# Moving the small tiles of a decoder kernel into an SBUF pool of their own, so that all large tiles start at multiples of 64 bytes

## The chip, the cores and the metric

The kernel runs on one core of one Trainium2 chip. The metric is the device time of one execution in microseconds; three executions of the kernel before gave a median of 2481.26 us (2479.68 to 2482.8).

## The reference

A small decoder: one retention layer and one latent-attention layer, each followed by a squared-ReLU MLP, for 256 tokens of width 2048 in float32. Of its work nearly all is in large matrix products with weights that are read once from HBM:

```python
def retention(h, w_in, w_out, cos, sin):
    ...
    proj = h @ w_in
    q, k, v, gate = jnp.split(proj, [H * dk, 2 * H * dk, 2 * H * dk + H * dv], axis=-1)
    ...
    return (jax.nn.silu(gate) * o) @ w_out
...
def sq_relu_mlp(h, w1, w2):
    return jnp.square(jax.nn.relu(h @ w1)) @ w2
...
    for layer in range(DEPTH):
        if layer < N_A_LAYERS:
            h = rms_norm(x, norm_mix[layer])
            x = x + retention(h, ret_w_in[layer], ret_w_out[layer], ret_cos, ret_sin)
        else:
            j = layer - N_A_LAYERS
            if j == 0:
                k_nope, k_pe, v = mla_shared_kv(rms_norm(x, kv_norm_in), mla_w_kv_down, mla_kv_norm,
                                                mla_w_kv_up, mla_k_nope_norm, mla_k_pe_norm,
                                                mla_cos, mla_sin)
            h = rms_norm(x, norm_mix[layer])
            x = x + mla_attention(h, mla_w_dq[j], mla_q_norm[j], mla_w_uq[j], mla_q_nope_norm[j],
                                  mla_q_pe_norm[j], mla_w_o[j], k_nope, k_pe, v, mla_cos, mla_sin)
        x = x + sq_relu_mlp(rms_norm(x, norm_mlp[layer]), mlp_w1[layer], mlp_w2[layer])
    return x
```

`w_in` is 2048 x 12288, `w_out` 4096 x 2048, each MLP 2048 x 8192 and 8192 x 2048. The rotary tables, the retention's decayed scores and the softmax attention are in the parts left out.

## The kernel before

**Number format.** TensorE multiplies in fp32r. To keep float32 accuracy each operand is split into a high part and the rest (`split`): ScalarE rounds (`CAST` to `wh`), VectorE subtracts (`TENSOR_TENSOR` to `wl`), and a product is three matmuls: high by high, high by low, low by high. Activations are split the same way into tiles called `act` (their names in the profile: a, y, n, hid, ckv, cq, ot, and those with `_more` for sums).

**Stages in order.** Retention: eight heads, each with the projections rq, rk (`gemm_t`) and rg, rv or rp (gate and value), then the output product ro; MLP 0 (u is the product with w1, d the one with w2); the shared keys and values kd, ku; the query products dq, dqp, uq; the attention output wo, wop; MLP 1 (u and d again). Most products are 2x2 block products (`gemm_pair`, `quad`). Some chunks of them use seven products instead of eight, with sums of weights that VectorE makes into buffers `us` (u_u, d_u, rp_u).

**Flow of the weights.** Each chunk of 1 MB goes by a DMA that SyncE issues into one of three `raw` buffers of 8 KB per partition, is split half by half into one of five `wh` and one of five `wl` buffers of 4 KB, and is used from there. `wh` and `wl` are the *moving* operand of the matmul, 512 columns at a time; a 128 x 128 piece of an `act` tile is the *stationary* one, its weights. In `gemm_t` it is the other way round: there `act` moves.

**What sets the order.** All operations are recorded first (`Plan.record`); a list scheduler then puts them in order by cost tables and due times, chooses buffers, and emits them all from one line, L421. So every instruction of the profile carries L421 and is told apart by tile names.

**Where tiles lie.** `nc.tile` makes a tile only when its first instruction is emitted. A tile with a tag gets one of the tag's buffers; each buffer is a slot of the SBUF pool, and slots follow each other in the order of their first use, each rounded up to 32 bytes. In the kernel before, one pool `sb` holds everything: the large tiles, the 36 small buffers of 32 bytes (`small`), and odd ones: `gains` (392 bytes), `pos_i` and `pos_f` (8 bytes), `neg_half` (64 bytes), `gqn` (4 bytes). So the large slots start at multiples of 32 bytes, and some 32-byte slots between them shift what follows.

Of the kernel before, what the change touches and what calls it, by code (L numbers as in the profile page):

```python
# [11 lines left out]
F32 = mybir.dt.float32  # L12
F32R = mybir.dt.float32r
BF16 = mybir.dt.bfloat16
I32 = mybir.dt.int32
# [436 lines left out]
P = 128  # L452
NT = 2
# [17 lines left out]
G_CKV, G_CQ, G_KN, G_QN, G_ALL = 80, 84, 96, 97, 98  # L471
# [6 lines left out]
def _pi_parts():  # L478
    two_pi = 2 * PI
    c1 = round(two_pi * 2**9) / 2**9  # L480
    c2 = round((two_pi - c1) * 2**23) / 2**23
    return c1, c2, two_pi - c1 - c2
# [3 lines left out]
def yoco(ctx: ExitStack, tc: tile.TileContext, a):  # L486
    nc = Plan(tc.nc, tc)
    pool = ctx.enter_context(tc.tile_pool(name="sb", bufs=1))
    psum = ctx.enter_context(tc.tile_pool(name="ps", bufs=1, space=PSUM))

    def f2k(shape, name, dtype=F32):
        return nc.tile(pool, [P, *shape], dtype, name, "f2k", 14)

    def small(w, name):
        return nc.tile(pool, [P, w], F32, name, "small", 36)

    def shaped(t, shape):
        v = t[:, : math.prod(shape)]
# [32 lines left out]
            run_first()  # L531


    gains = nc.tile(pool, [P, G_ALL], F32, "gains")
    cst = nc.tile(pool, [P, C_ALL], F32, "cst")
    pos_i = nc.tile(pool, [P, NT], I32, "pos_i")
    gpe = nc.tile(pool, [P, 2 * ROPE], F32, "gpe")
    nc.scalar.dma_start(gains, a["gains"])
    ident = cst[:, C_ID : C_ID + P]
    mask = cst[:, C_MASK : C_MASK + 3 * P]  # L540
    neg_half = nc.tile(pool, [P, 16], F32, "neg_half")
    nc.gpsimd.memset(neg_half, -0.5)
    warm = small(1, "warm")
    nc.scalar.copy(warm, neg_half[:, 0:1])

# [61 lines left out]
    def rstd(total, n, w, name):  # L607

        m = small(w, f"{name}_m")
        nc.gpsimd.tensor_scalar(m, total, 1.0 / n, EPS, op0=ALU.mult, op1=ALU.add)  # L610
        r = small(w, f"{name}_r")
        nc.gpsimd.tensor_tensor(r, m, neg_half[:, :w], op=ALU.pow)
        return r
# [363 lines left out]


    c1, c2, c3 = _pi_parts()
    pos_f = nc.tile(pool, [P, NT], F32, "pos_f")  # L980

    def sincos(inv, w, name):

# [43 lines left out]
    scale = (NOPE + ROPE) ** -0.5  # L1027
    rope_tab = nc.tile(pool, [P, 2, S], F32, "rope_tab")
    pe_tabs = [[nc.tile(pool, [P, 2, ROPE], F32, f"petab{t}{i}") for i in range(2)] for t in range(NT)]
    gqn = nc.tile(pool, [P, 1], F32, "gqn")  # L1030

    def mla_tables():
        sm = mla_sc[0](no_turn[0])
# [698 lines left out]
```

## Time and profile before

| | |
|---|---|
| Median of three executions | 2481.26 us |
| The profiled execution | 2479.39 us |
| Its span, first to last instruction | 2477.6 us |
| ScalarE busy | 1739.1 us (70%) |
| GpSimd busy | 248.1 us (10%) |
| Granted TensorE clock | 0.999 |
| HBM read, written | 479.14 MB, 39.85 MB |

"Busy" is the time in which an engine runs an instruction. For TensorE the ends of matmuls are modelled and they overlap: the page gives a 512-column matmul some 395 ns, though the next one begins much sooner. The pace of TensorE is therefore read from starts, that is from the count of matmuls in a stretch of time. PE is the matmul itself, PEld the loading of its weights.

### The profile page before, as it was taken

How to read it: one execution, taken by the hardware profiler on the slowest of the kernel's cores; microseconds unless marked ns; L12 is line 12 of the kernel's file. 1: busy time of each engine (PE TensorE's matmuls, PEld its weight loads, DVE VectorE, ACT ScalarE, POOL GpSimd, SP SyncE). 2: the span in 40 equal slices, each digit the busy share in tenths (PEclk: the TensorE clock that was granted, in tenths of full speed). 3: DMA queues.
4: the chain of work that ended last, by engine and by line, in shares of the span. 5: the costliest groups of instructions: out<-in, count | busy, mean ns of one | idle time of the engine just before them, and what ended most of it. 6: DMA issues, size and time to landing. Idle time of an engine off the chain costs nothing.

```text
span 2477.6 us, 31762 instructions
## 1 busy us (share of the span) xinstructions
PE 2465.7 (100%) x11406; PEld 2035.9 (82%) x11406; DVE 2240.7 (90%) x2959; ACT 1739.1 (70%) x2457; POOL 248.1 (10%) x287
## 2 busy tenths in 40 slices
PE   9999999999999999999999999999999999999999
PEld 7888888888888888888888788998888788888887
DVE  6899999888899999999999998777899899999999
ACT  6666666666667858668668777677678677586684
POOL 6510001000000010010110001111000100100100
PEclk9999999999999999999999999999999999999999
DMA  9566679666565697696887555445556976977874
GB/s 336 187 196 214 197 209 243 199 201 217 197 235 196 202 259 229 205 263 201 235 274 207 196 201 186 156 147 178 202 206 200 251 224 209 261 224 213 263 235 156
DMA packets 143742, 533.12 MB, mean 215 GB/s; under 512 B 61152, under 2 KB 62560, under 8 KB 90336
## 3 DMA queue, kind: packets, MB, share of 16 engines
q1 hardware_dynamic: 122192, 484.90, 58.7%
q0 software_dynamic: 21248, 46.15, 9.6%
q8 instruction: 89, 1.46, 0.2%
q14 instruction: 69, 0.57, 0.1%
q10 hardware_dynamic: 144, 0.05, 0.0%
HBM read 479.14 MB, written 39.85 MB: 209 GB/s over the span
## 4 chain that ended last, share of the span: by engine, by line
PE 96%; DVE 2%; DMA 1%; ACT 1%; issue 1%; SPq 0%; DVEq 0%; ACTq 0%
PE d_c L421 20%; PE u_c L421 20%; PE rp_c L421 8%; PE u_p L421 7%; PE ro_c L421 6%; PE d_p L421 6%; PE uq_acc L421 4%; PE rk_acc L421 4%; PE rq_acc L421 4%; PE rp_p L421 3%; PE ku_acc L421 2%; PE wo_acc L421 2%; PE ro_p L421 1%; PE wop_c L421 1%; PE dqp_c L421 1%; PE rg_acc L421 1%
## 5 line engine op out<-in xcount | busy, mean ns | idle before, releaser
L421 PE MATMUL d_c<-d_wh,hid 128*128 128x512 f32 x1412 | 464.4, 396 | 0.0
L421 PE MATMUL u_c<-u_wh,n 128*128 128x512 f32 x1328 | 435.6, 394 | 0.0
L421 PEld LDWEIGHTS d_c<-d_wh,hid 128*128 128x128 f32 x1412 | 265.2, 188 | 62.3 <-ACT d_wh L421 0.2
L421 PEld LDWEIGHTS u_c<-u_wh,n 128*128 128x128 f32 x1328 | 249.3, 188 | 58.2
L421 ACT CAST u_wh<-u_raw 128x1024 fp32r<-128x1024 f32 (+1 forms) x256 | 237.4, 952 | 79.8 <-PE u_c L421 59.6
L421 DVE TENSOR_TENSOR d_wl<-d_raw,d_wh 128x1024 fp32r<-128x1024 f32 (+1 forms) x256 | 281.4, 1110 | 6.2 <-ACT d_wh L421 5.6
L421 DVE TENSOR_TENSOR u_wl<-u_raw,u_wh 128x1024 fp32r<-128x1024 f32 (+1 forms) x256 | 275.3, 1095 | 10.6 <-ACT u_wh L421 9.6
L421 PE MATMUL d_c<-d_wl,hid 128*128 128x512 f32 x706 | 278.7, 395 | 0.0
L421 ACT CAST d_wh<-d_raw 128x1024 fp32r<-128x1024 f32 (+1 forms) x256 | 242.2, 966 | 33.4 <-PE d_c L421 17.4
L421 PE MATMUL u_c<-u_wl,n 128*128 128x512 f32 x664 | 261.7, 394 | 1.0 <-DVE u_wl L421 1.0
L421 ACT CAST d_wh<-d_u 128x1024 fp32r<-128x1024 f32 x106 | 108.5, 1048 | 142.5 <-DVE d_u L421 140.6
L421 ACT CAST u_wh<-u_u 128x1024 fp32r<-128x1024 f32 x120 | 123.7, 1051 | 97.1 <-DVE u_u L421 77.8
L421 PE MATMUL rp_c<-rp_wh,a 128*128 128x512 f32 x560 | 183.0, 393 | 0.0
L421 DVE TENSOR_TENSOR u_wl<-u_u,u_wh 128x1024 fp32r<-128x1024 f32 x120 | 143.9, 1221 | 23.8 <-ACT u_wh L421 23.8
L421 PEld LDWEIGHTS d_c<-d_wl,hid 128*128 128x128 f32 x706 | 132.7, 188 | 31.5 <-DVE d_wl L421 0.7
L421 PEld LDWEIGHTS u_c<-u_wl,n 128*128 128x128 f32 x664 | 124.7, 188 | 30.3 <-DVE u_wl L421 1.5
L421 ACT CAST rp_wh<-rp_raw 128x1024 fp32r<-128x1024 f32 x112 | 103.5, 943 | 62.7 <-PE rp_c L421 36.7
L421 DVE TENSOR_TENSOR d_wl<-d_u,d_wh 128x1024 fp32r<-128x1024 f32 x106 | 126.8, 1221 | 14.3 <-ACT d_wh L421 14.3
L421 DVE TENSOR_TENSOR rp_wl<-rp_raw,rp_wh 128x1024 fp32r<-128x1024 f32 x112 | 119.6, 1094 | 7.4 <-ACT rp_wh L421 7.0
L421 PEld LDWEIGHTS rp_c<-rp_wh,a 128*128 128x128 f32 x560 | 105.1, 188 | 24.8 <-DVE rk_u L421 0.9
L421 PE MATMUL u_p<-u_wh,n_more 128*128 128x512 f32 x360 | 122.6, 395 | 0.0
L421 PE MATMUL ro_c<-ro_wh,y 128*128 128x512 f32 x368 | 120.0, 396 | 0.0
(479 smaller groups left out, 5946.3 us busy)
## 6 DMA issues: line engine op xcount, KB each, us to landing
u_raw<-in_mlp_w SPq DMA_DIRECT2D x128, 1024.0 KB, 6.2
d_raw<-in_mlp_w SPq DMA_DIRECT2D x128, 1024.0 KB, 5.0
rp_raw<-in_ret_w_gv SPq DMA_DIRECT2D x56, 1024.0 KB, 5.1
ro_raw<-in_ret_w_out SPq DMA_DIRECT2D x32, 1024.0 KB, 5.3
uq_raw<-in_mla_w_uq SPq DMA_DIRECT2D x24, 768.0 KB, 4.2
rq_raw<-in_ret_w_qk SPq DMA_DIRECT2D x16, 1024.0 KB, 6.2
rk_raw<-in_ret_w_qk SPq DMA_DIRECT2D x16, 1024.0 KB, 4.9
xh<-d_c POOLq DMA_DIRECT2D x48, 256.0 KB, 6.3
```

The lines of the kernel that those rows point to most:

```text
L421: op.made = fn(*(real(v) for v in op.args), **{k: real(v) for k, v in op.kw.items()})
```

## The change

It makes a second pool `few` for the 36 small buffers and for `pos_i`, `pos_f`, `neg_half` and `gqn`, and makes `gains` 112 columns wide instead of 98 (448 bytes instead of 392), of which the added 14 are not used:

```diff
     pool = ctx.enter_context(tc.tile_pool(name="sb", bufs=1))
+    few = ctx.enter_context(tc.tile_pool(name="few", bufs=1))
...
     def small(w, name):
-        return nc.tile(pool, [P, w], F32, name, "small", 36)
+        return nc.tile(few, [P, w], F32, name, "small", 36)
...
-    gains = nc.tile(pool, [P, G_ALL], F32, "gains")
+    gains = nc.tile(pool, [P, G_ALL + 14], F32, "gains")
     cst = nc.tile(pool, [P, C_ALL], F32, "cst")
-    pos_i = nc.tile(pool, [P, NT], I32, "pos_i")
+    pos_i = nc.tile(few, [P, NT], I32, "pos_i")
...
-    nc.scalar.dma_start(gains, a["gains"])
+    nc.scalar.dma_start(gains[:, :G_ALL], a["gains"])
...
-    neg_half = nc.tile(pool, [P, 16], F32, "neg_half")
+    neg_half = nc.tile(few, [P, 16], F32, "neg_half")
...
-    pos_f = nc.tile(pool, [P, NT], F32, "pos_f")
+    pos_f = nc.tile(few, [P, NT], F32, "pos_f")
...
-    gqn = nc.tile(pool, [P, 1], F32, "gqn")
+    gqn = nc.tile(few, [P, 1], F32, "gqn")
```

The built program has the same instructions in the same order on every engine, with the same waits; the two differ in addresses alone. The byte in its partition at which each large slot starts, in both built programs (in brackets: modulo 256):

| Slots | Before | After |
|---|---|---|
| raw | 20704 (224), 33056 (32), 57632 (32) | 20672, 32960, 57536 (192 each) |
| wh | 43296 (32), 67872 (32), 86848 (64), 99136 (64), 111424 (64) | 43200, 67776, 86720, 99008, 111296 (192 each) |
| wl | 53536 (32), 76064 (32), 90944 (64), 103232 (64), 119616 (64) | 53440, 75968, 90816, 103104, 119488 (192 each) |
| us | 183296 (0), 187392 (0) | 182976, 187072 (192 each) |
| act, 24 slots | 2 at (32), 6 at (64), 6 at (96), 2 at (0), 1 at (128), 7 at (192) | 24 at (192) |
| f2k, 14 slots | 1 at (0), 7 at (32), 6 at (96) | 14 at (192) |

Within a slot a matmul's moving operand starts at a multiple of 2,048 bytes and its stationary one at a multiple of 512.

## The prediction

> **What bounds the kernel now.** I read the page first, then the list of TensorE's waits, then the busy time in stretches of 60 us, and at last short stretches in which every matmul has its operands in known places.
>
> ```profile
> span 2477.6 us, 31762 instructions
> PE 2465.7 (100%) x11406; PEld 2035.9 (82%) x11406; DVE 2240.7 (90%) x2959; ACT 1739.1 (70%) x2457; POOL 248.1 (10%) x287
> PE 96%; DVE 2%; DMA 1%; ACT 1%; issue 1%; SPq 0%; DVEq 0%; ACTq 0%
> ...
> PE idle L421 <- DVE zeros L421: 1.2, 1, 1.2
> PE u_c L421 <- DVE u_wl L421: 1.0, 1, 1.0
> PE rg_acc L421 <- ACT a L421: 0.9, 1, 0.9
> PE d_p L421 <- DVE n L421: 0.7, 1, 0.7
> ```
>
> TensorE is busy for 2465.7 of 2477.6 us and holds 96% of the chain that ended last; its longest wait for anyone is 1.2 us (columns: total us, times, longest). So TensorE's own pace sets the time, and a change counts by what it does to the distance from one matmul to the next. Nearly all of that work is of one form: 9,412 matmuls of 512 columns in fp32r, 8,883 of which have neighbours of the same form (the built program counts them). The other 529 alternate with 256-column ones in the rq and rk projections.
>
> **What the change can touch.** No instruction is added, removed or moved, and no wait changes. Only start addresses do. VectorE and ScalarE show no sign of caring: the raw buffers never begin at a multiple of 64 bytes before the change, the buffers called u always do, and the same operation takes the same time from either.
>
> ```profile
> L421 DVE TENSOR_TENSOR d_wl<-d_raw,d_wh 128x1024 fp32r<-128x1024 f32 x203 | 245.0, 1221 | 6.2 <-ACT d_wh L421 5.6
> L421 DVE TENSOR_TENSOR d_wl<-d_u,d_wh 128x1024 fp32r<-128x1024 f32 x106 | 126.8, 1221 | 14.3 <-ACT d_wh L421 14.3
> L421 ACT CAST d_wh<-d_raw 128x1024 fp32r<-128x1024 f32 x203 | 210.8, 1056 | 32.4 <-PE d_c L421 17.1 <-issue 7.8 <-ACT d_wh L421 3.5
> L421 ACT CAST d_wh<-d_u 128x1024 fp32r<-128x1024 f32 x106 | 108.5, 1048 | 142.5 <-DVE d_u L421 140.6 <-PE d_c L421 0.8
> ```
>
> 1221 against 1221 ns, and 1056 against 1048. For the two elementwise engines I take zero; the bound from these rows is 8 ns on a cast, and ScalarE, 70% busy, would hide that. The 36 small tiles, pos_i, pos_f, gqn and neg_half are read as scalars beside long work; their move I cost at nothing too.
>
> TensorE is another matter. While a matmul streams its moving operand, the weights of the next one are being loaded:
>
> ```profile
> 880.07 0.39 PE L421 MATMUL d_c<-d_wl,hid 128*128 128x512 f32 x1
> 880.07 0.42 PEld L421 LDWEIGHTS d_c<-d_wh,hid 128*128 128x128 f32 x2
> ```
>
> Both begin at 880.07. So I compared, for every matmul, where its moving operand starts with where the *next* one's weights start. Before the change the difference modulo 256 bytes is 0 for 1,707 of the 8,883, 64 for 387, 128 for 1,400, 192 for 1,077, and no multiple of 64 for 4,312. The windows view shows unbroken stretches of one kind (columns: stretch, sum, busy us of PE with its matmul records, clock, DMA share, GB/s; x counts also the records still running at the edges). By the trace's own start times the numbers that begin inside them are, in this order, 29 and 29 (difference 0), 21 (the end of the first of these), 36 and 26 (no multiple of 64), 26 (128), 24 (192) and 24 (64).
>
> ```profile
> 801.21:807.81 6.60, 6.60 (x30) 1.00 0.73 206
> 2428.33:2434.93 6.60, 6.60 (x30) 1.00 0.68 223
> 803.05:807.81 4.76, 4.76 (x22) 1.00 0.85 260
> 251.72:260.12 8.40, 8.40 (x38) 1.00 0.60 157
> 2419.25:2425.31 6.06, 6.06 (x28) 1.00 0.56 181
> 344.23:350.29 6.06, 6.06 (x27) 1.00 0.56 188
> 899.15:904.74 5.59, 5.59 (x26) 1.00 0.89 223
> 2353.71:2359.20 5.49, 5.49 (x25) 1.00 0.90 316
> ```
>
> Divide: 6.60/29 = 227.6 ns where the two starts agree, and 4.76/21 = 226.7 once such a stretch has run for eight matmuls. 8.40/36 = 233.3, 6.06/26 = 233.1, 6.06/26 = 233.1 and 5.59/24 = 232.9 for the other kinds, 5.49/24 = 228.8 for a difference of 64. The granted clock is 1.00 in all of them, so it is no throttle, and the stretches lie in early and late stages alike. All stretches of at least 12 matmuls say the same: 49 with difference 0 lie around 228.1 ns, 231 of the three slow kinds around 233. After the change the built program has difference 0 in all 8,883 places: the pool rounds slots to 32 bytes, every size left in it is a multiple of 64 and the long ones of 512, so everything large starts at 192 modulo 256. That is more than the change's words say.
>
> **The sum.** Slow kinds: 4,312 + 1,400 + 1,077 = 6,789 matmuls, each from about 233.1 to about 227.3 ns (between the 227.6 of a whole stretch and the settled 226.7, since a transposition or a 256-column matmul still breaks a stretch now and then): 6,789 x 5.8 ns = 39 us. The 2,094 quick ones gain about 1 ns each by being broken off less often: 2 us. Together 41 us of TensorE time. A second way to the same number, from whole stretches of 60 us:
>
> ```profile
> 840.00:900.00 60.00, 60.00 (x260) 48.45 (x259) 56.28 (x63) 38.00 (x48) 7.83 (x9) 1.00 0.80 230
> 1200.00:1260.00 60.00, 60.00 (x260) 48.52 (x259) 56.64 (x62) 36.43 (x42) 10.35 (x12) 1.00 0.92 250
> 2100.00:2160.00 60.00, 60.00 (x261) 48.61 (x260) 56.43 (x61) 34.66 (x40) 10.39 (x12) 1.00 0.94 263
> 2040.00:2100.00 60.00, 60.00 (x268) 48.63 (x267) 58.86 (x78) 49.70 (x70) 1.72 (x2) 1.00 0.67 206
> 2220.00:2280.00 60.00, 60.00 (x268) 48.81 (x267) 59.45 (x76) 44.73 (x61) 3.64 (x5) 1.00 0.67 207
> 2400.00:2460.00 60.00, 60.00 (x260) 48.62 (x259) 59.12 (x74) 40.14 (x51) 0.00 (x0) 1.00 0.51 180
> ```
>
> (Columns: PE, PEld, DVE, ACT, POOL, clock, DMA share, GB/s.) The first three hold 512-column matmuls alone: 60.00/259 = 231.7 ns on average over all kinds. 8,883 x (231.7 - 227.3) = 39 us. I take 40.
>
> What does not shrink with it: VectorE. It has 58.86, 59.45 and 59.12 us of work in three of these stretches, and TensorE wants to pass each in about 60 x 227.3/231.7 = 58.9 us. There 0.6 + 0.2 us cannot be had; elsewhere VectorE has 3 to 4 us free per 60. Then DMA: its share is 0.92 and 0.94 in two of the stretches and would rise by 2%. A transfer is late already now and then:
>
> ```profile
> DMA  9566679666565697696887555445556976977874
> ...
> DVE u_u L421 <- DMA u_raw<-in_mlp_w: 8.2, 11, 3.5
> ACT u_wh L421 <- PE u_c L421: 76.9, 86, 1.8
> ```
>
> 11 waits, 8.2 us in all, which reach TensorE once, for 1.0 us. The page's DMA row has six of 40 slices at 0.9 or more; if those gained nothing, that would be 6 x 1.1 = 7 us; if they gained in full, 0. I take 1 us for VectorE and 1 for DMA. The last row says why so little: 86 times ScalarE stood waiting for TensorE to free a buffer, so most of the chain behind it speeds up along with TensorE. Forecast: 40 - 2 = 38 us off the profiled execution's own 2479.4 us, 2441.4. The median of the three timed runs is 2481.26, 1.9 us above that execution; put on the median's footing, it is **2443 us**.
>
> Here the Trainium skill speaks against the change. "TensorE: Matmul & The Clock Gate", section "Step-by-step: what each phase is for", says that TensorE has two independent SBUF read ports and that "Loading the next tile's weights doesn't steal SBUF read bandwidth from the running matmul." By that sentence the two starts could not matter to each other, and the time would stay at 2481. The trace does not agree with it: 227.6 ns where the starts agree, 233 where they don't.
>
> **Rivals.** (a) *Nothing happens*: the stretches differ for another reason that goes with the slots, say which engine happens to write beside them. For it: slots and places in a gemm go together, since the scheduler hands them out in order. Against it: three differences that share no cause with each other (128, 192, odd) have the same 233, and 0 and 64 the same 227 to 229, in retention and in both MLPs. Time: 2481.
>
> (b) *VectorE becomes the bound*. It is the next engine, 90% busy over the span and 56.3 to 59.5 us of 60 in the stretches quoted. If in practice it cannot be packed closer than it is there, the MLPs (780 to 1440 and 1800 to the end, 1338 of 2478 us) gain nothing and only the rest does: 1140/2478 x 40 = 18 us, 2463 on the median's footing. For it: 59.45. Against it: that same 59.45 shows that it can be packed to 99%, and the stretch at 1200 would need 56.64/58.9 = 96%.
>
> (c) *The absolute start counts and 192 is a bad one*: slower. Before the change no moving operand of a 512-column matmul starts at 192 modulo 256, so the traces show the pair (192, 192) nowhere; the quick stretches quoted above all have 64 with 64, and others 32 with 32. If what matters were a fixed set of good starts instead of agreement, all 8,883 would run at 233.3: 8,883 x (233.3 - 231.7) = +14 us, 2495. It would decide in the very first gemm: a stretch of 24 matmuls takes 5.60 us there or it takes 5.45. Against it: a stream of 512 columns runs through 2,048 bytes, eight times round 256, so a common start can hardly matter by itself.
>
> (d) *The change doesn't do what it says*: the built program shows that it does, so I give it nothing.
>
> **How the numbers follow.** Forecast 0.68, (b) 0.20, (a) 0.07, (c) 0.05. The lower end is all 8,883 at the settled 226.7 (8,883 x 5.0 = 44 us) with nothing lost, and 4 us for the 1,889 fp32r matmuls that I cost at nothing (529 beside 256-column ones and 1,360 narrower; 2 ns each is a guess): 2433. The upper end takes in most of (b): 2464. A measurement of this kernel tells about 0.2%, 5 us, from no change; faster by more than that are the forecast and (b), 0.88; within it (a), 0.07; slower (c), 0.05.
>
> **What would show it.** Right: the three stretches with 512-column matmuls alone hold 263 to 265 records instead of 260; any stretch of 24 takes 5.44 to 5.48 us; VectorE's instructions keep 1221 ns; its share rises from 90% to about 92%; TensorE's waits stay in single microseconds. (b) would show as TensorE waits for u_wl and d_wl of some 20 us in sum; (c) as 233 ns everywhere with the differences equal. I would be wrong in the step from stretches to the whole if equal starts gave 227 ns only in some gemms.

## The result and the profile after

| | Median, us | Range, us | Ratio to before | 95% interval |
|---|---|---|---|---|
| before, 4 executions | 2480.47 | 2479.58 to 2482.8 | | |
| after, 4 executions | 2445.17 | 2442.36 to 2446.53 | 0.9855 | 0.9838 to 0.9872 |

By the medians the change makes the kernel 35.3 us faster; by the ratio it takes 1.45% less time (1.28 to 1.62%). The forecast was 2443, its range 2433 to 2464.

First the page of the kernel after: the span, the busy time of each engine, and the shares of the chain that ended last.

```profile
span 2444.6 us, 31762 instructions
PE 2425.8 (99%) x11406; PEld 2032.9 (83%) x11406; DVE 2231.6 (91%) x2959; ACT 1732.1 (71%) x2457; POOL 251.6 (10%) x287
PE 70%; DVE 17%; ACT 4%; DMA 4%; issue 3%; SPq 0%; DVEq 0%; ACTq 0%
```

The same 31,762 instructions take 33.0 us less in the profiled executions (2479.39 and 2446.41 us; the spans differ by as much). TensorE's busy time falls by 2465.7 - 2425.8 = 39.9 us, and the rest of the span, in which TensorE does nothing, grows from 2477.6 - 2465.7 = 11.9 to 2444.6 - 2425.8 = 18.8 us, by 6.9. The two make the 33.0. The third line is the surprise: TensorE is busy for 99% of the span and yet holds only 70% of the chain, where it held 96%. VectorE now has 17% of it. The last section comes back to this.

Next the windows view of the kernel after (columns as in the prediction: stretch, sum, busy us of PE with its matmul records, clock, DMA share, GB/s). These are the same matmuls as in six of the stretches that the prediction shows, found by their place in the program. By the trace's start times 36, 26, 26, 24, 24 and 29 begin in them.

```profile
252.18:260.36 8.18, 8.18 (x38) 1.00 0.63 156
2387.44:2393.34 5.90, 5.90 (x28) 1.00 0.55 186
343.45:349.35 5.90, 5.90 (x28) 1.00 0.58 186
890.75:896.19 5.44, 5.44 (x26) 1.00 0.94 232
2319.72:2325.16 5.44, 5.44 (x26) 1.00 0.89 338
795.09:801.66 6.57, 6.57 (x31) 1.00 0.84 213
```

8.18/36 = 227.2 ns where it was 233.3; 5.90/26 = 226.9 where it was 233.1, twice; 5.44/24 = 226.7 where it was 232.9; 226.7 where it was 228.8; and 6.57/29 = 226.6 where it was 227.6. In these stretches the kinds of before are gone, in retention and in both MLPs alike.

The same in long stretches (windows view, all engines: PE, PEld, DVE, ACT, POOL, clock, DMA share, GB/s):

```profile
840.00:900.00 60.00, 60.00 (x266) 49.69 (x265) 57.16 (x65) 39.34 (x49) 8.69 (x10) 1.00 0.88 249
1200.00:1260.00 60.00, 60.00 (x266) 49.68 (x265) 56.33 (x61) 36.11 (x43) 11.78 (x16) 1.00 0.95 270
2100.00:2160.00 60.00, 59.11 (x261) 48.61 (x260) 56.12 (x62) 38.57 (x47) 6.94 (x8) 1.00 0.82 248
2340.00:2400.00 60.00, 57.87 (x262) 47.33 (x261) 58.23 (x77) 52.98 (x76) 0.00 (x0) 1.00 0.61 197
```

The first three are those in which the prediction expected 263 to 265 records instead of 260 or 261. Two hold 266. The third holds 261 as before, chiefly because TensorE stands still in it for 60.00 - 59.11 = 0.9 us. In the last TensorE loses 2.1 us, in one wait of some 1.5 us for ScalarE (`u_c`) and one of some 0.7 for VectorE (`u_wl`). Before the change it lost nothing between the same two times:

```profile
2340.00:2400.00 60.00, 60.00 (x267) 48.56 (x266) 56.57 (x69) 53.11 (x74) 3.40 (x7) 1.00 0.81 250
```

So there the gain is given back. (The work between these two times is not quite the same, since the kernel after is further on by then.) TensorE's waits by name (total us, times, longest), kernel after:

```profile
PE hid_tp L421 <- ACT u_c L421: 2.8, 5, 1.5
PE u_c L421 <- DVE u_wl L421: 2.7, 4, 0.9
PE rp_p L421 <- DVE rp_wl L421: 1.4, 2, 1.1
PE idle L421 <- DVE zeros L421: 1.2, 1, 1.2
```

The largest total was 1.2 us before. Now the first two are 2.8 and 2.7, still single microseconds, but behind ScalarE and VectorE, not behind the start of the program. What stands behind the 0.9 us at 2100 is seen in the chain of waits between 2118 and 2145 us of the kernel after (columns: start, length, what):

```profile
2118.44 2.28 DVE u_wl L421 x2
2120.72 0.02 issue
2120.74 8.47 DMA u_raw<-in_mlp_w
...
2129.30 1.24 DVE u_u L421
...
2131.17 2.36 DVE u_wl L421 x2
2133.54 0.02 issue
2133.55 5.41 DMA u_raw<-in_mlp_w
...
2139.05 1.24 DVE u_u L421
```

It is a circle: VectorE finishes the last read of a raw buffer, the next chunk of weights is loaded into it (8.47 and 5.41 us), and VectorE takes the sum u_u from it. The `u_wl` at 2131.17 comes behind the first of these sums, and TensorE, idle for 0.89 us, begins the matmul that reads it at 2132.44. VectorE's waits for such loads are 9.2 us in 13 times, where they were 8.2 in 11:

```profile
DVE u_u L421 <- DMA u_raw<-in_mlp_w: 9.2, 13, 2.7
```

VectorE's two commonest large instructions of the d product keep their length within 5 ns of 1221 (groups by line of the kernel after: busy us, mean ns):

```profile
L421 DVE TENSOR_TENSOR d_wl<-d_raw,d_wh 128x1024 fp32r<-128x1024 f32 x203 | 243.4, 1216 | 0.0
L421 DVE TENSOR_TENSOR d_wl<-d_u,d_wh 128x1024 fp32r<-128x1024 f32 x106 | 126.5, 1218 | 14.3 <-ACT d_wh L421 14.3
```

### The profile page after: what moved, and what is told of

It reads as the page before. It is cut to its first block, busy times and chain, and to the rows that moved or that the text cites. A ratio compares the mean times of both kernels' runs of the same rounds, so it can differ in the third digit from the quotient of the medians.

```text
span 2444.6 us, 31762 instructions
## 1 busy us (share of the span) xinstructions
PE 2425.8 (99%) x11406; PEld 2032.9 (83%) x11406; DVE 2231.6 (91%) x2959; ACT 1732.1 (71%) x2457; POOL 251.6 (10%) x287
## 4 chain that ended last, share of the span: by engine, by line
PE 70%; DVE 17%; ACT 4%; DMA 4%; issue 3%; SPq 0%; DVEq 0%; ACTq 0%
PE u_c L421 13%; PE d_c L421 12%; PE rp_c L421 7%; DVE d_wl L421 5%; PE uq_acc L421 4%; PE u_p L421 4%; PE d_p L421 4%; PE rk_acc L421 4%; PE rq_acc L421 3%; PE ro_c L421 3%; DVE u_wl L421 3%; PE rp_p L421 2%; DVE d_u L421 2%; DMA u_raw<-in_mlp_w 2%; PE wo_acc L421 2%
## 5 line engine op out<-in xcount | busy, mean ns | idle before, releaser
L421 PE MATMUL d_c<-d_wh,hid 128*128 128x512 f32 x1412 | 457.2, 391 | 0.0
L421 PE MATMUL u_c<-u_wh,n 128*128 128x512 f32 x1328 | 429.5, 389 | 0.0
L421 DVE TENSOR_TENSOR u_wl<-u_u,u_wh 128x1024 fp32r<-128x1024 f32 x120 | 143.3, 1219 | 20.2 <-ACT u_wh L421 20.1
L421 DVE TENSOR_TENSOR d_wl<-d_u,d_wh 128x1024 fp32r<-128x1024 f32 x106 | 126.5, 1218 | 14.3 <-ACT d_wh L421 14.3
L421 POOL DMA_DIRECT2D xh<-d_c x48 | 41.6, 867 | 752.1 <-DVE d_wl L421 446.1
```

What stands on the lines that cost most here:

```text
L421: op.made = fn(*(real(v) for v in op.args), **{k: real(v) for k, v in op.kw.items()})
```

## The experiments

The theory: the time from one 512-column matmul to the next is set by the moving operand's start against the start of the next matmul's weights, modulo 256 bytes. Its rivals: multiples of 64 bytes are good in themselves, as the change's words suggest; some absolute starts are good or bad; the slots only go together with something else. All eight kernels of the first three parts have the instructions, order and waits of the change, and differ from it in addresses alone.

**1. The two halves of the change.** `few_only` keeps the second pool and drops the padding of `gains`. All large tiles then begin at 160 modulo 256, which is no multiple of 64, but all agree with each other.

```diff
-    gains = nc.tile(pool, [P, G_ALL + 14], F32, "gains")
+    gains = nc.tile(pool, [P, G_ALL], F32, "gains")
```

> The pool for small tiles alone, gains not padded: every large tile starts at 160 modulo 256, no multiple of 64 at all, but all of them alike. Theory (the moving operand's start and the next weights' start must agree modulo 256): as fast as the change, 2445 us, stretches at 226.7 ns a matmul. Rival (a start must be a multiple of 64): back to 2480 us, 233 ns. Rival (192 modulo 256 is a good absolute start): slower than 2445 too.

`pad_only` keeps the padding and puts everything back into one pool; the differences are then those of the kernel before.

```diff
-        return nc.tile(few, [P, w], F32, name, "small", 36)
+        return nc.tile(pool, [P, w], F32, name, "small", 36)
...
-    pos_i = nc.tile(few, [P, NT], I32, "pos_i")
+    pos_i = nc.tile(pool, [P, NT], I32, "pos_i")
...
```

> The padding of gains alone, the small tiles left in the one pool. All starts are other ones than before, but the differences stand exactly as before the change: 0 in 1,707 places, 64 in 387, 128 in 1,400, 192 in 1,077, no multiple of 64 in 4,312. Theory of agreement: the time of the kernel before, 2481 us, within 3 us. Rival (the change's two parts add up, the padding gives its share): something between, about 2460 to 2470 us.

| | Median, us | Ratio to before | 95% interval |
|---|---|---|---|
| few_only | 2443.78 | 0.9846 | 0.983 to 0.9862 |
| pad_only | 2480.88 | 0.9999 | 0.9989 to 1.0008 |

The second pool alone does all of it, without a multiple of 64 anywhere; the padding alone does nothing. pad_only keeps even the kinds of the kernel before, stretch by stretch (windows view of pad_only; 24, 29 and 24 matmuls begin in these):

```profile
900.61:906.19 5.58, 5.58 (x26) 1.00 0.90 236
802.67:809.27 6.60, 6.60 (x30) 1.00 0.73 207
2354.15:2359.64 5.49, 5.49 (x25) 1.00 0.91 350
```

5.58/24 = 232.5, 6.60/29 = 227.6 and 5.49/24 = 228.8 ns; before they were 232.9, 227.6 and 228.8.

**2. One difference for all.** `wh` and `wl` go into a pool `mv` of their own at the start, so that all of them begin at 128 modulo 256; whether `gains` (448 bytes) and `cst` lie in front of the other tiles or in `few` decides where those begin. So nearly all of the 8,883 matmuls get one difference: 0 in all for d0, 64 in 8,806 for d64, 128 in 8,812 for d128, 192 in 8,806 for d192. In these four everything large begins at a multiple of 64 bytes. `d96` is d64 with `gains` unpadded: 8,806 at 96.

```diff
+    mv = ctx.enter_context(tc.tile_pool(name="mv", bufs=1))
     pool = ctx.enter_context(tc.tile_pool(name="sb", bufs=1))
...
-            wh = nc.tile(pool, [P, 1024], F32R, f"{name}_wh{part}", "wh", 5)
-            wl = nc.tile(pool, [P, 1024], F32R, f"{name}_wl{part}", "wl", 5)
+            wh = nc.tile(mv, [P, 1024], F32R, f"{name}_wh{part}", "wh", 5)
+            wl = nc.tile(mv, [P, 1024], F32R, f"{name}_wl{part}", "wl", 5)
...
-    gains = nc.tile(pool, [P, G_ALL + 14], F32, "gains")
-    cst = nc.tile(pool, [P, C_ALL], F32, "cst")
+    gains = nc.tile(few, [P, G_ALL + 14], F32, "gains")
+    cst = nc.tile(few, [P, C_ALL], F32, "cst")
```

(This is d0. d64 has only `cst` in `few`, d128 only `gains`, d192 neither.)

> wh and wl in a pool of their own at 128 modulo 256, all other large tiles also at 128 (gains and cst moved out of their pool): all starts multiples of 64, difference 0. It is the control of the next three, which have the same pools. Both theories: 2445 us; rival of an absolute start at 192: slower.

> As the control, but gains in the main pool: wh and wl at 128, the others at 64 modulo 256, difference 64 in 8,806 places, all multiples of 64. Theory of agreement: 228.8 to 229.2 ns a matmul as in the stretches of that kind before the change, 8,806 x 2 = 18 us more, less a few us of waits: 2459 us. Rival (multiples of 64 suffice): 2445 us.

> As the control, but cst back in the main pool: wh and wl at 128, all other large tiles at 0 modulo 256, every one a multiple of 64, difference 128 in 8,812 of 8,883 places. Theory of agreement: 8,812 x (233.0 - 227.0) = 53 us more, less the 8 us or so of TensorE's waits that a slower TensorE no longer has: 2490 us, slower than the kernel before. Rival (multiples of 64 suffice): 2445 us.

> As the control d0, with gains and cst in the main pool: wh and wl at 128, the others at 192 modulo 256, difference 192 in 8,806 places, all multiples of 64. Theory of agreement: as slow as d128 or 0.5 ns a matmul slower, 2485 to 2491 us. Rival (multiples of 64 suffice): 2445 us.

> As the control d0, with cst in the small tiles' pool and gains unpadded in the main one: wh and wl at 128, the others at 32 modulo 256, difference 96 in 8,806 places: the fifth point of the series. Theory of agreement: 233 ns a matmul as in the stretches of no multiple of 64 before the change, 2485 to 2491 us, like d128 and d192. Rival (only the parity of multiples of 64 against 32 counts, and 128 and 192 are slow for a reason of their own): no time between is excluded; it would lie apart from 2485 to 2492 us.

| | Median, us | Ratio to before | 95% interval |
|---|---|---|---|
| d0 | 2443.28 | 0.9846 | 0.9831 to 0.986 |
| d64 | 2457.53 | 0.9906 | 0.9891 to 0.9921 |
| d128 | 2485.07 | 1.0016 | 1.0007 to 1.0026 |
| d192 | 2492.08 | 1.0039 | 1.0026 to 1.0052 |
| d96 | 2490.26 | 1.0035 | 1.0023 to 1.0047 |

One stretch shows the cause: the 24 matmuls that took 5.59 us before and 5.44 after. A fence for each kernel's windows view, in the order d0, d64, d128, d192, d96:

```profile
889.72:895.15 5.43, 5.43 (x25) 1.00 0.96 255
```

```profile
894.36:899.86 5.50, 5.50 (x26) 1.00 0.83 206
```

```profile
902.69:908.27 5.58, 5.58 (x26) 1.00 0.95 275
```

```profile
904.68:910.28 5.60, 5.60 (x26) 1.00 0.88 230
```

```profile
905.27:910.87 5.60, 5.60 (x25) 1.00 1.00 263
```

Divided by 24: 226.3, 229.2, 232.5, 233.3 and 233.3 ns, with the clock at 1.00 in all. Times 8,800 matmuls the last four are 26, 55, 62 and 62 us above d0; the medians are 14, 42, 49 and 47 above it. Both put d64 nearest, then d128, then d192 and d96 within their spread, but all distances of the medians are smaller, by 12 to 15 us. Part of that is d0's idle time of TensorE: span minus busy time by the pages is 20.1 us in d0 and 14.5, 11.4, 14.9 and 15.5 in the others, 5 to 9 less. The rest is finer than so short a stretch can tell: 0.01 us on 24 matmuls is 0.4 ns, and that is 4 us on 8,800. Over the whole trace, by the start times of the 512-column matmuls between two of their kind (without the intervals over 260 ns), the averages are 227.0, 229.0, 232.4, 233.3 and 233.3 ns. Times 8,800 the last four are 18, 48, 55 and 55 us above d0; less the 5 to 9 us of idle time that is 12, 39, 50 and 51, against 14, 42, 49 and 47 by the medians. So the pace and the idle time account for the five kernels within 4 us.

What follows: a multiple of 64 bytes is not what counts, since d0, d64, d128 and d192 all have it and lie 49 us apart. The absolute start doesn't count either: agreement at 160 (few_only), at 128 (d0) and at 192 (the change) gives 2443.8, 2443.3 and 2445.2. And nothing that goes with slots or places in a product counts, since those are the same in all. Of the sizes expected, d128 is 5 us faster than the 2490 and d192 1 us slower than the upper end of its 2485 to 2491; d64 and d96 are as expected within 2 us.

The page "TensorE: Matmul & The Clock Gate" of the Trainium skill, section "Step-by-step: what each phase is for", says that loading the next weights takes no read bandwidth from the running matmul. If that were all that passes between the two, these five kernels would take one time. They don't: the same matmuls and the same weight loads, which differ only in where they start, take 233.3 instead of 226.3 ns. What inside the chip costs the difference, no run here shows.

**3. Two differences in one kernel.** In `wl128` only `wl` lies in `mv`, at 128; all else is at 0. Of the 8,883, 2,943 have a difference of 128 and 5,940 have 0. Of three matmuls in turn one is slow by its own pair of starts.

```diff
-            wl = nc.tile(pool, [P, 1024], F32R, f"{name}_wl{part}", "wl", 5)
+            wl = nc.tile(mv, [P, 1024], F32R, f"{name}_wl{part}", "wl", 5)
...
-    gains = nc.tile(pool, [P, G_ALL + 14], F32, "gains")
+    gains = nc.tile(few, [P, G_ALL + 14], F32, "gains")
```

> Only wl in a pool of its own, at 128 modulo 256, everything else at 0: all multiples of 64; every third matmul (2,943 of 8,883) has the difference 128, the two between have 0. If each matmul pays for its own difference alone: 2,943 x (232.4 - 227.0) = 16 us more, about 2459 us. If the quick pace has to settle over several matmuls (before the change the first of a quick stretch took 232.7 ns, the second 230.8, and 226.7 came after eight), nearly all are slow: 8,883 x (231.6 - 227.0) = 41 us more less 8 us of waits, about 2478 us. Rival (multiples of 64 suffice): 2445 us.

It took 2488.74 us, ratio 1.0028 with an interval of 1.0018 to 1.0037: slower than both times that the expectation gives, and slower than the kernel before. Windows view of wl128, the same 24 and 29 matmuls as above:

```profile
903.41:909.01 5.60, 5.60 (x26) 1.00 0.97 287
805.14:811.91 6.77, 6.77 (x31) 1.00 0.75 206
```

5.60/24 = 233.3 and 6.77/29 = 233.4 ns. So two thirds of the matmuls, which have the good difference, run no faster than the rest. By start times over the whole trace the ones with `wl` moving take 233.6 ns, the `wh` after it 230.3, the other `wh` 235.0. The simple rule, that each matmul pays for its own pair of starts, falls here: what holds is that a sequence is fast if all its pairs agree. How far a bad pair reaches, these runs don't show. Nor do they show that it is the *next* matmul's weights that must agree, and not the matmul's own: in the kernels of part 2 both differences are the same in all but 14 of 8,782 places at most, in wl128 in all, and in the kernel before in 8,055 of 8,752. Where they part there, it is slow either way: 232.4 ns on average where only the next weights agree (134 matmuls), 231.2 where only the own do (145), 228.7 where both do. What the series shows is that moving and stationary tiles must start alike modulo 256 bytes.

**4. What took the rest.** The prediction counted 2 us of new waits; the page shows 6.9 more idle time of TensorE. `less_dve` asks whether VectorE sets them. It is the change with the 64 sums u_c cut from 512 to 64 columns, so it leaves out 448 of the 512 columns of these sums. (The built program has 8 waiting instructions more, 31,770 in all; the matmuls are the same.)

```diff
-                nc.vector.tensor_tensor(block[0], block[0], block[1], op=ALU.add)
+                nc.vector.tensor_tensor(block[0], block[0], block[1], op=ALU.add).cut = cut
...
+                if op.cut:
+                    args = [v[:, : op.cut] for v in args]
...
-                c = summed(c)
+                c = summed(c, 64)
```

> The change, with 64 additions on VectorE in the up projections (u_c += u_p and the like, 512 columns) cut to 64 columns, in the same order: some 0.47 us less each, 30 us of VectorE in the MLPs. The part left out: 448 of 512 columns of those sums. Theory (the 10 us of gain that are missing are TensorE's new waits for VectorE, directly and through ScalarE's relu): the waits for hid_tp and u_wl, 7.7 us together, fall to some 2 us, 2439 to 2441 us. Rival (they come from late DMAs or from a pace that VectorE doesn't set): 2445 us, the waits stay.

`after_again` is the change unaltered, as the measure beside it and beside the next.

> The change once more, on the chip and in the hour of the next kernel: 2443 to 2447 us, TensorE's waits as in its first profile.

| | Median, us | Ratio to before | 95% interval |
|---|---|---|---|
| less_dve | 2443.09 | 0.9843 | 0.9828 to 0.9858 |
| after_again | 2444.32 | 0.9851 | 0.9837 to 0.9864 |

Page of less_dve, busy time and chain:

```profile
PE 2422.9 (99%) x11406; PEld 2031.9 (83%) x11406; DVE 2207.9 (90%) x2959; ACT 1733.2 (71%) x2457; POOL 250.0 (10%) x287
PE 77%; DVE 12%; DMA 4%; ACT 4%; issue 2%; SPq 1%; POOL 0%; DVEq 0%; ACTq 0%
```

23.7 us less work for VectorE brought 1.2 us, and the intervals overlap. Its span is 2442.3, so TensorE stands idle for 2442.3 - 2422.9 = 19.4 us, as after the change (18.8). The 7.7 us of waits that the expectation names are hid_tp and u_wl with the two for rp_wl (2.8 + 2.7 + 1.4 + 0.8); in less_dve the four are 1.9, 2.5, 1.5 and 0.9, 6.8 us, and not the 2 us of the theory. The time lies between the two answers, but the waits stay, as the rival has it: VectorE's amount of work in these sums is not what sets the new waits. What sets them is open: the loads of raw in the circle above are the next suspect, but a kernel with fewer bytes or more raw buffers was not tried.

`pool_sums` asks the other way round whether VectorE can be relieved by an engine that is idle for 90% of the time: two of the three sums of activations go from VectorE to GpSimd. Here the list scheduler also puts some operations in another order.

```diff
-        nc.vector.tensor_tensor(sums[:, 2], sums[:, 1], blocks[:, 0], op=ALU.subtract)
-        nc.vector.tensor_tensor(sums[:, 3], blocks[:, 2], sums[:, 2], op=ALU.add)
+        nc.gpsimd.tensor_tensor(sums[:, 2], sums[:, 1], blocks[:, 0], op=ALU.subtract)
+        nc.gpsimd.tensor_tensor(sums[:, 3], blocks[:, 2], sums[:, 2], op=ALU.add)
```

> The change, with two of the three additions in each with_sums (128x128, 0.28 us on VectorE, some 100 of them) given to GpSimd, which is busy for 10%: 29 us less for VectorE; the planner reorders a little. Theory (VectorE's load makes TensorE's waits): the waits fall by some 5 us, 2440 us. Rival 1 (the waits are set elsewhere): 2445 us. Rival 2 (GpSimd and VectorE hinder each other, or the sums come too late for TensorE): slower than 2445 us.

2477.66 us, ratio 0.9984 (0.9975 to 0.9992): 33 us slower than after_again. The chain of sums is now long (groups by line of pool_sums):

```profile
L421 POOL TENSOR_TENSOR hid_sum<-hid_sum,hid_u 128x128 f32<-128x128 f32 x32 | 74.1, 2316 | 584.1 <-DVE hid_sum L421 367.7 <-ACT u_c L421 166.1 <-ACT d_wh L421 50.3
L421 POOL TENSOR_TENSOR hid_sum<-hid_u,hid_sum 128x128 f32<-128x128 f32 x32 | 28.4, 889 | 2.5
```

On VectorE the same two take 286 and 287 ns in the kernel before:

```profile
L421 DVE TENSOR_TENSOR hid_sum<-hid_u,hid_sum 128x128 f32<-128x128 f32 x32 | 9.2, 287 | 0.0
L421 DVE TENSOR_TENSOR hid_sum<-hid_sum,hid_u 128x128 f32<-128x128 f32 x32 | 9.2, 286 | 0.0
```

By these rows each pair takes 2316 + 889 - 573 = 2632 ns longer (GpSimd's spans are rough in this profile), in front of ScalarE's rounding, which stands before the product d. List of waits of pool_sums:

```profile
PE d_c L421 <- DVE d_wl L421: 8.6, 15, 1.9
PE d_c L421 <- ACT hid_more L421: 8.4, 8, 1.1
ACT hid_more L421 <- POOL hid_sum L421: 66.3, 16, 5.6
```

ScalarE stands for 66.3 us waiting for the sums, TensorE for ScalarE and VectorE behind it. VectorE's busy time did fall, to 2224.5 us, and it bought nothing: of the three answers expected, the second rival, in which the sums come too late for TensorE, is the one that came. Against the change's profile the span is longer by 31.7 us (2476.3), of which 19.1 are idle time of TensorE and 12.6 its busy time.

No version that computes everything beat the change beyond the spread: few_only and d0 lie 1.4 and 1.9 us below it, within each other's ranges.

## Why the prediction was right

**What bounds the kernel** was right: nothing but start addresses changed, and the time followed TensorE's pace.

**The rule of the two starts** was right, as far as the change needs it: the six stretches followed went to 226.6 to 227.2 ns. The 24 matmuls took 5.44 us (5.44 to 5.48 foretold). Of the three 60-us stretches two hold 266 records (263 to 265 foretold) and the third 261, because of a wait. As a rule for each matmul by itself it was too simple; wl128 shows that. And that the weights in question are the next matmul's is not shown. Neither did harm, since after the change all 8,883 agree with the next weights and with their own.

**The first term**, 40 us of TensorE time, was some 4 us too small. By start times the 512-column matmuls went from 232.1 to 227.0 ns on average in unbroken stretches; 8,883 x 5.1 = 45 us. The prediction had 231.7 ns before the change, because it divided 60 us by 259 records, though by start times 258, 258 and 259 matmuls begin in its three stretches. The 512-column matmuls beside 256-column ones, which it put at nothing, took 1.6 us more (the change of their summed start-to-start times). That leaves some 44 us. The page's busy time falls by only 39.9: the page has a matmul run for some 395 ns though the next one begins after 227, so the first part of a wait counts as busy there.

**The second term**, 2 us of waits, was the one mis-sized: it measured 6.9 us by the page's idle time and 10.9 us by start times. I had allowed 1 us for three stretches in which VectorE is full and 1 for late transfers. The loss comes in more small waits. Among the 8,883 matmuls the intervals to the next start that are longer than 260 ns went from 86 (32.5 us) to 110 (44.9 us), and 24 more at the usual 0.227 would be 5.4 of these 12.4 us, so 7.0 are waiting. Behind transpositions, which otherwise keep 98 ns, seven intervals are so long (4.8 us) where one was (0.3 us), and all their intervals together grew by 3.9 us.

The two terms by start times make 44 - 10.9 = 33 us, and the profiled executions differ by 33.0; the medians by 35.3. The forecast of 38 lies so near because a gain 4 us too small and a loss 9 us too small work against each other. That part is luck.

The other kernels bear out that the quickest pace has the most idle time. Span minus busy time of TensorE is 20.1 us in d0, 20.0 in few_only and 18.8 after, but 13.9 in pad_only, 14.6 in wl128 and 11.4 to 15.5 in d64 to d96, where it does not follow the pace any further. VectorE as the bound, rival (b), would have shown as 20 us of waits for u_wl and d_wl; they are 2.7 and 0.2.

**Rivals (a) and (c)** fall by the runs, not by the result alone: d0 to d192 have the same slots in the same places and lie 49 us apart, and a common start at 128, 160 or 192 is equally good.

**VectorE's lengths** were to stay at 1221 ns and came out as 1216 and 1218; its share is 91%, with 92 foretold. That is 9 us less busy time in 2,240, which I can't explain and which lies off the sum.

## What to carry to other kernels

Before padding tiles to a round number, find out from the trace what two addresses have to agree: here it was the starts of the moving and of the stationary operand modulo 256 bytes, and a pool in which no odd size lies between the large tiles settles it for all (here all sizes behind the two tables at its start are multiples of 256 bytes). Test such a rule with a series that sets one difference for everything; among the multiples of 64 alone it spread this kernel over 2443 to 2492 us. When the bound engine gets quicker by 2%, count what waits for it: its idle time went from 12 to 19 us here though no other engine was given more work.

## What was not expected of the hardware

- The cost of a difference is not symmetric: a moving start 64 bytes past the weights' gives about 229 ns, one of 192 (64 the other way) 233.3, as bad as 96 and a little worse than 128 at 232.5 (part 2).
- A mixed sequence is slow as a whole (wl128: 233.3 ns in a stretch with two thirds of the pairs in agreement), and the kernel with it is slower than the one before, in which 1,707 of 8,883 agree in unbroken groups.
- A chain of waits can mislead about a bound: TensorE holds 96% of it before, 94% in d128, 88% in d64 and 70% after (76% in after_again, the same kernel), although it is busy for 99% of the span or more in all; perhaps because the chain crosses over more often to VectorE and the loads when these are on TensorE's heels, which was not tested. Page of d64 and of d128:

```profile
PE 88%; DVE 5%; DMA 3%; ACT 2%; issue 2%; SPq 0%; DVEq 0%; ACTq 0%
```

```profile
PE 94%; DVE 3%; ACT 1%; DMA 1%; issue 1%; SPq 0%; DVEq 0%; ACTq 0%
```
